# Attention scores from stacked high and low parts: two fp32r matmuls in place of one fp32 matmul on 64 rows

## The chip, the cores and the metric

The kernel runs on one core of one Trainium2 chip. The metric is the device time of one execution in microseconds (us), as the median of the runs of a kernel; less is better.

## What is computed

Two layers of a diffusion backbone over 256 context tokens and 256 latent tokens of width 1024. The even layer runs differential softmax attention (4 heads, two score maps of 64 features per head) beside a gated linear attention (GLA, 4 heads, forward and backward); the odd layer runs a gated scan (HGRN2); each layer ends in a SwiGLU feed-forward. The part that the change touches is this, for each head:

```python
aq = rms_norm(aq.reshape(Bn, L, A_HEADS, 2, A_DQK), qk_gain[0])
ak = rms_norm(ak.reshape(Bn, L, A_HEADS, 2, A_DQK), qk_gain[1])
ql = apply_axial_rope(ql, rope_cos, rope_sin)
kl = apply_axial_rope(kl, rope_cos, rope_sin)
...
s = jnp.einsum('bqhcd,bkhcd->bhcqk', q, k).astype(F32) * (A_DQK ** -0.5)
p = jax.nn.softmax(s, axis=-1)
a = (p[:, :, 0] - lam * p[:, :, 1]).astype(v.dtype)
return jnp.einsum('bhqk,bkhe->bqhe', a, v)
```

Context queries see the 256 context keys, latent queries see all 512 keys.

## The kernel before

All 512 tokens lie along the free axis and features lie on the 128 rows. Dense projections are done in three fp32r matmuls per 128x128 block of weights (`mm3`): high part of the weight times high part of the activation, high times low, low times high. A weight piece of 128x1024 arrives by one DMA, ScalarE (ACT) casts its high part (L269), VectorE (DVE) subtracts to get the low part (L270). All matmuls are recorded on one line, L117, and nearly all activations on L71, so the rows below are told apart by tile names.

The even layer's mixer is written as `qk_tile` for q and k of head 0, `gla_pair(0)`, the value projection, and then for each head `qk_tile(0, hd)`, `qk_tile(1, hd)` and `attn_head(hd)`, with pieces of the modulation (`ada`) between, then `gla_pair(1)` and four gate projections `gs` (L803). A scheduler sets the order of all instructions on each engine from this text before the run, so heads, GLA and dense work are interleaved; on the chip every engine then works through its own list in that order.

- `qk_tile` (L720 to L736) normalises a projected 128x512 tile by its root mean square (tile `qsq`, matmul with `blk64`), applies the rotation to the 256 latent tokens on VectorE (L730 to L735) and leaves the tile in fp32. Rows 0 to 63 are score map 0, rows 64 to 127 are score map 1. Each of the eight q and k tiles has its own buffer, tags `x0` to `x7`, which held the input tokens before and will hold them again (`load_x`) for the residual.
- `attn_head` (L742 to L778) goes over context and latent queries (`s`), two blocks of 128 queries (`qb`) and two score maps (`c`). A score tile is one matmul on the 64 rows of its map, into a PSUM bank of which there are two (tag `s`). VectorE takes the maximum (L757), ScalarE the exponential with its sum (tile `p`), VectorE combines both maps (L765, L766), TensorE transposes (`t_ps`, L770) and multiplies with the values (`oa_ps`).
- `head_post` (tiles `hsq`, `ms_ps`, L606) normalises a head's output: square on ScalarE, a sum over rows on TensorE (`ms_ps`), Ln and Exp on ScalarE, a product on VectorE. There is one `hsq` buffer for all eight heads.
- The gates `gs` pass through Silu only after every Exp and Ln before them (class `Act`), because the two need different function tables; a table load stands between. Then `ob` is multiplied by `gs` (L811), split into high and low parts (`oH`, `oL`, L628 and L629) and multiplied with the output weights. The output projection goes over the four attention heads first and then over the four GLA heads.

Of the kernel before, what the change touches and what calls it, by code (L numbers as in the profile page):

```python
# [10 lines left out]
F32 = mybir.dt.float32  # L11
F32R = mybir.dt.float32r
U32 = mybir.dt.uint32
AF = mybir.ActivationFunctionType
ALU = mybir.AluOpType
# [3 lines left out]
P = 128  # L19
# [3 lines left out]
T = 512  # L23
# [27 lines left out]
def hybrid_kernel(ctx: ExitStack, tc: tile.TileContext, A, out, dbg=None):  # L51
    nc = tc.nc
    PE, V = nc.tensor, nc.vector
# [34 lines left out]
    S = Act()  # L88

    def pool(es, name, bufs, **kw):  # L90
        kw.setdefault("reuse_waits", "tile")
        return es.enter_context(tc.tile_pool(name=name, bufs=bufs, **kw))

    cst = pool(ctx, "cst", 1)
    xp = pool(ctx, "xp", 1)
# [8 lines left out]
    def dma(o, i):  # L104
        nc.sync.dma_start(out=o, in_=i)
# [6 lines left out]
    def dump(name, ap):  # L112
        if dbg is not None and name in dbg:
            dma(dbg[name], ap)

    def mm(o, l, r, start, stop):
        return PE.matmul(out=o, lhsT=l, rhs=r, start=start, stop=stop)  # L117

    def mtile(name, tag):
        return pm.tile([P, 512], F32, name=name, tag=tag, bufs=1 if tag == "t" else 2)  # L120
# [5 lines left out]
    x = {}  # L126
# [127 lines left out]
    def rstd_from_ms(o, ps, n):  # L254

        S.activation(out=o, in_=ps, func=AF.Ln, scale=1.0 / n, bias=eps_t)
        S.activation(out=o, in_=o, func=AF.Exp, scale=-0.5)
# [39 lines left out]
    def dense_group(fl, outs, rhs, ks, per_bank=1, extra=0, tag="t", extra1=0):  # L297

        ada(extra, tag)
        ada1(extra1)  # L300
        for i, k in enumerate(ks):
            for j, o in enumerate(outs):
                wH, wL = fl.nxt()
                mm3(o, wH, wL, rhs[k][0], rhs[k][1], i == 0 and j % per_bank == 0,
                    i == len(ks) - 1 and j % per_bank == per_bank - 1)
# [48 lines left out]
    def dtile():  # L354
        return pd.tile([P, 512], F32, name="d", tag="d")
# [242 lines left out]
    def head_post(pp, o, src, n, gain, tag):  # L598

        sq = pp.tile([P, n], F32, name="hsq", tag="hsq", bufs=1)  # L600
        S.activation(out=sq, in_=src, func=AF.Square)
        ms = mtile("ms_ps", tag)
        mm(ms[:, 0:n], ones, sq, True, True)
        rsd = sq
        rstd_from_ms(rsd, ms[:, 0:n], P)
        V.scalar_tensor_tensor(out=o, in0=src, scalar=gain, in1=rsd, op0=ALU.mult, op1=ALU.mult)  # L606
# [110 lines left out]
    qT = {}  # L717
    kT = {}

    def qk_tile(which, hd, ps=None):  # L720
        if ps is None:
            ps = dtile()
            dense_group(fl, [ps], h, range(KT))
        rsd = ppool.tile([P, T], F32, name="qsq", tag="qsq", bufs=1)
        S.activation(out=rsd, in_=ps, func=AF.Square)
        ms = dtile()
        mm(ms, blk64, rsd, True, True)
        rstd_from_ms(rsd, ms, 64)
        t = xp.tile([P, T], F32, name=f"qk{which}{hd}", tag=f"x{2 * hd + which}")
        V.scalar_tensor_tensor(out=t, in0=ps, scalar=qkg[:, which:which + 1], in1=rsd, op0=ALU.mult, op1=ALU.mult)  # L730
        sh = ppool.tile([P, 256], F32, name="sh", tag="sh")
        V.stream_shuffle(out=sh, in_=t[:, 256:512], mask=[(i + 16) % 32 for i in range(32)])
        V.tensor_tensor(out=sh, in0=sh, in1=rope[:, 1, :], op=ALU.mult)
        V.tensor_tensor(out=t[:, 256:512], in0=t[:, 256:512], in1=rope[:, 0, :], op=ALU.mult)
        V.tensor_tensor(out=t[:, 256:512], in0=t[:, 256:512], in1=sh, op=ALU.add)  # L735
        return t  # L736

    def put_vA(t, ps):
        vA[t] = bigp.tile([P, 512], F32, name=f"vA{t}")
# [2 lines left out]
    def attn_head(hd):  # L742
        q, k = qT[hd], kT[hd]
        oa = bigp.tile([P, T], F32, name=f"oa{hd}")
        for s in range(2):
            nk = 2 + 2 * s
            nkeys = nk * P
            aT = ppool.tile([P, nk, 256], F32, name="aT", tag=f"aT{s}", bufs=1)
            for qb in range(2):
                q0 = s * 256 + qb * P  # L750
                st = ppool.tile([P, 6], F32, name="st", tag="st")
                pr = []
                for c in range(2):
                    r = slice(64 * c, 64 * c + 64)
                    sp_ = mtile("s_ps", "s")
                    mm(sp_[:, 0:nkeys], q[r, q0:q0 + P], k[r, 0:nkeys], True, True)
                    V.tensor_reduce(out=st[:, c:c + 1], in_=sp_[:, 0:nkeys], axis=AX.X, op=ALU.max)  # L757
                    V.tensor_scalar(out=st[:, c:c + 1], in0=st[:, c:c + 1], scalar1=-0.125, scalar2=None, op0=ALU.mult)
                    pt = ppool.tile([P, 512], F32, name=f"p{c}", tag=f"p{c}")
                    S.activation(out=pt[:, 0:nkeys], in_=sp_[:, 0:nkeys], func=AF.Exp, scale=0.125,  # L760
                                 bias=st[:, c:c + 1], accum_out=st[:, 2 + c:3 + c])
                    pr.append(pt)
                V.reciprocal(out=st[:, 4:6], in_=st[:, 2:4])
                V.tensor_scalar(out=st[:, 5:6], in0=st[:, 5:6], scalar1=neglam, scalar2=None, op0=ALU.mult)
                V.tensor_scalar(out=pr[0][:, 0:nkeys], in0=pr[0][:, 0:nkeys], scalar1=st[:, 4:5], scalar2=None, op0=ALU.mult)  # L765
                V.scalar_tensor_tensor(out=pr[0][:, 0:nkeys], in0=pr[1][:, 0:nkeys], scalar=st[:, 5:6],  # L766
                                       in1=pr[0][:, 0:nkeys], op0=ALU.mult, op1=ALU.add)
                tp = mtile("t_ps", "t")
                for kt in range(nk):
                    PE.transpose(tp[:, kt * P:(kt + 1) * P], pr[0][:, kt * P:(kt + 1) * P], ident)  # L770
                S.copy(out=aT[:, 0:nk, qb * P:(qb + 1) * P],
                       in_=tp[:, 0:nkeys].rearrange("p (a b) -> p a b", a=nk))
            o = mtile("oa_ps", "t")
            for kt in range(nk):
                mm(o[:, 0:256], vA[kt][:, hd * P:(hd + 1) * P], aT[:, kt, :], kt == 0, kt == nk - 1)
            S.copy(out=oa[:, s * 256:(s + 1) * 256], in_=o[:, 0:256])
        head_post(ppool, oa, oa, T, sgain, "t")
        return oa  # L778

    oa = {}  # L780
    qT[0] = qk_tile(0, 0, pss[4])
    kT[0] = qk_tile(1, 0, pss[5])
    gla_pair(0)
    dense_tokens(A["w_even_av"], h, put_vA)
    ada(2, "d")
    oa[0] = attn_head(0)
    for hd in range(1, 4):
        ada(1, "d")
        qT[hd] = qk_tile(0, hd)
        kT[hd] = qk_tile(1, hd)  # L790
        ada(1, "d")
        oa[hd] = attn_head(hd)
    dump("q1", qT[1])
    dump("oa1", oa[1])
    gla_pair(1)
    dump("ob1", ob[1])
# [138 lines left out]
    qs = bigp.tile([P, KT, 256], F32, name="qs")  # L935
# [365 lines left out]
```

## Time and profile before

| | us |
|---|---|
| median of 3 runs | 1174.69 |
| lowest and highest run | 1173.56, 1174.72 |
| the profiled execution | 1171.33 |
| its span in the trace | 1169.6 |
| TensorE (PE) busy | 1146.2 (98%) |
| PE weight loads (PEld) busy | 982.8 (84%) |
| VectorE (DVE) busy | 794.5 (68%) |
| ScalarE (ACT) busy | 546.6 (47%) |

PE's busy time is a union of modelled intervals, each with the latency of its matmul, so 98% does not mean that the array works at its peak. In the timeline the difference between the starts of two neighbouring matmuls tells what one really takes. The even layer's mixer with the attention lies between about 90 and 345 us of the span.

### The profile page before, as it was taken

To read this page: it belongs to the slowest core of one execution; us is meant where nothing else is said; L and a number is where in the kernel's file an instruction comes from. 1 tells how busy PE (TensorE), PEld (TensorE's weight loads), DVE (VectorE), ACT (ScalarE), POOL (GpSimd) and SP (SyncE) were. 2 spreads that over 40 slices of the span, in tenths; PEclk is the share of its full clock that TensorE was granted. 3 is DMA by queue.
4 is the path that set the end of the run, shared out by engine and by line. 5 is a ranking of instruction groups with operands and counts; after the bars stand their busy time and mean duration, and the time that the engine had idled before them with its cause. 6 is when DMAs were issued, how large, how long until landed. Compare 5 with 4: busy or idle time off the path is not lost. (4 is left out here: it accounts for less than half of the span.)

```text
span 1169.6 us, 21851 instructions
## 1 busy us (share of the span) xinstructions
PE 1146.2 (98%) x8954; PEld 982.8 (84%) x8954; DVE 794.5 (68%) x1671; ACT 546.6 (47%) x952; POOL 0.2 (0%) x4
## 2 busy tenths in 40 slices
PE   8999999999999999999999999999999998999998
PEld 6777665666889888888888889999898988999998
DVE  3537856985767767666677637869899976655663
ACT  5436546754435222212222325958778865433432
POOL 0000000000000000000000000000000000000000
PEclk9999989999999999999999999999999999999999
DMA  9531432234423555555776422342221234555552
GB/s 356 211 116 36 146 127 82 100 127 146 178 74 105 167 178 171 159 174 179 252 238 232 161 90 70 129 145 92 73 91 61 87 127 129 183 191 178 185 181 91
DMA packets 50021, 170.19 MB, mean 146 GB/s; under 512 B 6528, under 2 KB 8064, under 8 KB 49792
## 3 DMA queue, kind: packets, MB, share of 16 engines
q1 hardware_dynamic: 49920, 168.79, 43.2%
q8 instruction: 70, 1.15, 0.4%
q14 instruction: 31, 0.25, 0.1%
HBM read 167.72 MB, written 1.05 MB: 144 GB/s over the span
## 5 line engine op out<-in xcount | busy, mean ns | idle before, releaser
L269 ACT CAST wH<-w 128x1024 fp32r<-128x1024 f32 x212 | 222.2, 1049 | 410.2 <-PE d L117 314.0
L117 PE MATMUL d<-hL,wH 128*128 128x256 f32 (+1 forms) x1152 | 386.7, 336 | 2.5 <-DVE hL L387 2.5
L117 PE MATMUL d<-hH,wH 128*128 128x256 f32 (+1 forms) x1152 | 382.4, 339 | 5.6 <-ACT hH L71 4.1
L117 PE MATMUL d<-hH,wL 128*128 128x256 f32 (+1 forms) x1152 | 385.3, 335 | 0.0
L270 DVE TENSOR_TENSOR wL<-w,wH 128x1024 fp32r<-128x1024 f32 x212 | 258.6, 1221 | 124.7 <-ACT wH L269 122.0
L117 PEld LDWEIGHTS d<-hH,wH 128*128 128x128 f32 x1152 | 218.3, 191 | 32.0 <-ACT hH L71 4.9
L117 PEld LDWEIGHTS d<-hL,wH 128*128 128x128 f32 x1152 | 220.6, 191 | 25.0 <-DVE hL L387 3.3
L117 PEld LDWEIGHTS d<-hH,wL 128*128 128x128 f32 x1152 | 220.1, 191 | 21.5
L117 PE MATMUL d<-gL,wH 128*128 128x256 f32 (+1 forms) x374 | 121.8, 327 | 0.0
L117 PE MATMUL d<-gH,wL 128*128 128x256 f32 (+1 forms) x374 | 121.7, 327 | 0.0
L117 PE MATMUL d<-gH,wH 128*128 128x256 f32 (+1 forms) x374 | 121.7, 327 | 0.0
L227 DVE SCALAR_TENSOR_TENSOR jk<-ada_w,scb 128x1024 bf16<-128x1024 f32 x80 | 97.7, 1222 | 2.2 <-DMA ada_w<-in_w_ada 0.8
L882 DVE TENSOR_TENSOR fs<-fs,d 128x256 f32<-128x256 f32 (+1 forms) x46 | 24.6, 536 | 77.4 <-PE d L117 75.8
L117 PEld LDWEIGHTS d<-gL,wH 128*128 128x128 f32 x374 | 71.1, 190 | 6.1
L117 PEld LDWEIGHTS d<-gH,wL 128*128 128x128 f32 x374 | 71.1, 190 | 6.0
L117 PEld LDWEIGHTS d<-gH,wH 128*128 128x128 f32 x374 | 71.0, 190 | 6.0
L117 PE MATMUL d<-wH,hH 128*128 128x256 f32 (+1 forms) x192 | 61.9, 323 | 0.0
L117 PE MATMUL d<-wL,hH 128*128 128x256 f32 (+1 forms) x192 | 61.6, 322 | 0.0
L117 PE MATMUL d<-wH,hL 128*128 128x256 f32 (+1 forms) x192 | 61.5, 321 | 0.0
L825 DVE SCALAR_TENSOR_TENSOR x<-d,modt,x 128x256 f32<-128x256 f32 x64 | 28.5, 480 | 42.4 <-PE d L117 42.4
L71 ACT ACTIVATE QK<-QK 128x512 f32<-128x512 f32 x72 | 42.6, 628 | 2.4 <-DVE QK L493 2.1
L117 PEld LDWEIGHTS a<-QK 128*32 128x32 f32 (+5 forms) x1408 | 33.8, 118 | 10.1 <-issue 6.3
(216 smaller groups left out, 1461.1 us busy)
## 6 DMA issues: line engine op xcount, KB each, us to landing
w<-in_w_ffn_in SPq DMA_DIRECT2D x88, 512.0 KB, 3.4
ada_w<-in_w_ada SPq DMA_DIRECT2D x80, 512.0 KB, 4.2
w<-in_w_ffn_out SPq DMA_DIRECT2D x44, 512.0 KB, 3.4
ada_w<-in_w_ada SPq DMA_DIRECT2D x8, 1024.0 KB, 9.4
w<-in_w_even_a SPq DMA_DIRECT2D x16, 512.0 KB, 4.8
w<-in_w_odd_f SPq DMA_DIRECT2D x16, 512.0 KB, 3.3
x<-in_xT SPq DMA_DIRECT2D x16, 256.0 KB, 3.7
w<-in_w_out_even SPq DMA_DIRECT2D x8, 512.0 KB, 3.5
```

The lines of the kernel that those rows point to most:

```text
L71: ins = nc.scalar.activation(**kw)
L117: return PE.matmul(out=o, lhsT=l, rhs=r, start=start, stop=stop)
L227: ins = V.scalar_tensor_tensor(out=jk, in0=w1[0], scalar=1.0, in1=scb[:, v, :], op0=ALU.mult, op1=ALU.mult, accum_out=modt[:, l, m, dt, v: ...
L269: S.copy(out=wH, in_=w)
L270: ins = V.tensor_tensor(out=wL, in0=w, in1=wH, op=ALU.subtract)
L825: tail[0] = V.scalar_tensor_tensor(out=xt[:, lo:hi], in0=ps[:, lo:hi], scalar=mods[l, m, k][:, v:v + 1], in1=xt[:, lo:hi], op0=ALU.mult, o ...
L882: V.tensor_tensor(out=s[:, lo:hi], in0=s[:, lo:hi], in1=pu, op=ALU.mult)
```

## The change

`qk_tile` no longer returns one fp32 tile. For q it makes, for each score map `c`, a 128-row fp32r tile `qs`: the high part (ACT cast) in the map's own 64 rows and the low part (DVE subtraction) in the other 64. For k it makes two tiles for each map: `kh` with the high part in both halves and `kl` with the low part in both halves. A score tile is then `qs` times `kh` plus `qs` times `kl`, two fp32r matmuls over all 128 rows, into the same PSUM bank: all four products of high and low parts are summed.

The tags move too. The fp32 tile has tag `x6` (q) or `x7` (k) for every head, and `qs`, `kh` and `kl` have tags `x0` to `x5`, again for every head: one buffer each where there was one per head.

```diff
-        t = xp.tile([P, T], F32, name=f"qk{which}{hd}", tag=f"x{2 * hd + which}")
+        t = xp.tile([P, T], F32, name=f"qk{which}{hd}", tag=f"x{6 + which}")
...
-        return t
+        parts = []
+        for c in range(2):
+            own, far = (slice(0, 64), slice(64, 128))[::1 - 2 * c]
+            if which == 0:
+                a = xp.tile([P, T], F32R, name=f"qs{c}", tag=f"x{c}")
+                S.copy(out=a[own], in_=t[own])
+                V.tensor_tensor(out=a[far], in0=t[own], in1=a[own], op=ALU.subtract)
+                parts.append(a)
+            else:
+                a = xp.tile([P, T], F32R, name=f"kh{c}", tag=f"x{2 + 2 * c}")
+                b = xp.tile([P, T], F32R, name=f"kl{c}", tag=f"x{3 + 2 * c}")
+                for r in (own, far):
+                    S.copy(out=a[r], in_=t[own])
+                for r in (own, far):
+                    V.tensor_tensor(out=b[r], in0=t[own], in1=a[own], op=ALU.subtract)
+                parts.append((a, b))
+        return parts
...
-                    r = slice(64 * c, 64 * c + 64)
                     sp_ = mtile("s_ps", "s")
-                    mm(sp_[:, 0:nkeys], q[r, q0:q0 + P], k[r, 0:nkeys], True, True)
+                    for i in range(2):
+                        mm(sp_[:, 0:nkeys], q[c][:, q0:q0 + P], k[c][i][:, 0:nkeys], i == 0, i == 1)
```

A debug dump of `qT[1]`, which this build doesn't make, goes as well. The scheduler sets a new order for the mixer; later parts stand as they stood. Three places of it matter below.

**The scores.** On TensorE, the last scores of head 0 (numbers tell buffers apart). Before:

```order
L117 MATMUL s_ps<-qk_875,qk_862 128x512
L117 MATMUL d<-hH_625,wH 128x512
L117 MATMUL d<-hL_626,wH 128x512
L117 MATMUL d<-hH_625,wL 128x512
L117 MATMUL s_ps<-qk_875,qk_862 128x512
```

Now:

```order
L117 MATMUL s_ps<-kh_888,qs_869 128x512
L117 MATMUL s_ps<-kl_889,qs_869 128x512
L117 MATMUL s_ps<-kh_894,qs_872 128x512
L117 MATMUL s_ps<-kl_895,qs_872 128x512
L117 MATMUL o_ps<-at,vB_832 128x256
```

Each tile is two matmuls; there are 64 in all, where there were 32.

**The subtractions.** On VectorE, inside the products of `gla_pair(0)`, ahead of the first scores. Before:

```order
L500 TENSOR_TENSOR QK<-QK,qkb_688 128x256
L504 TENSOR_TENSOR QK<-QK,qkb_688 128x256
L500 TENSOR_TENSOR QK<-QK,qkb_688 128x256 x2
L504 TENSOR_TENSOR QK<-QK,qkb_688 128x256
```

Now:

```order
L500 TENSOR_TENSOR QK<-QK,qkb_688 128x256
L504 TENSOR_TENSOR QK<-QK,qkb_688 128x256
L752 TENSOR_TENSOR kl_889<-qk_881,kh_888 64x512 x2
L752 TENSOR_TENSOR kl_895<-qk_881,kh_894 64x512 x2
L500 TENSOR_TENSOR QK<-QK,qkb_688 128x256 x2
```

Four subtractions for k of head 0 stand in the queue here; the two for its q stand some 25 instructions earlier. Each further head has six of its own.

**The end of the mixer.** On TensorE, the last sum of squares `ms_ps` (that of GLA head 3) and the output projection; `oH_3202` to `oL_3215` are attention heads 0 to 3. Before, where `ms_ps` stands after 8 of the 48 matmuls on attention heads, and 40 of them follow until the first on GLA head 0:

```order
L117 MATMUL d<-oH_3206,wH 128x512
L117 MATMUL d_3255<-oH_3206,wH 128x512
L117 MATMUL ms_ps<-hsq,ones 128x512
L117 MATMUL d<-oL_3207,wH 128x512
L117 MATMUL d<-oH_3206,wL 128x512
```

Now, where `oH_3318` is attention head 3 and `oH_3323` GLA head 0; `ms_ps` twice is GLA heads 2 and 3:

```order
L117 MATMUL d_3359<-oL_3319,wH 128x512
L117 MATMUL d_3359<-oH_3318,wL 128x512
L117 MATMUL ms_ps<-hsq,ones 128x512 x2
L117 MATMUL d<-oH_3323,wH 128x512 x3
L117 MATMUL d_3359<-oH_3323,wH 128x512
L117 MATMUL d<-oL_3324,wH 128x512
```

All 48 matmuls on attention heads now stand ahead of the two sums. What ScalarE has there now (`ob_854` and `ob_855` are GLA heads 2 and 3):

```order
L71 ACTIVATE hsq<-ob_854 128x512
L269 CAST wH<-w 128x1024
L71 ACTIVATE hsq<-ms_ps,eps_t 128x512
L71 ACTIVATE hsq<-hsq 128x512
L71 ACTIVATE hsq<-ob_855 128x512
L71 ACTIVATE hsq<-ms_ps,eps_t 128x512
L71 ACTIVATE hsq<-hsq 128x512
L71 ACT_TABLE_LOAD
L71 ACTIVATE gs_3046<-gs_3046 128x512
```

The square of head 3 (`hsq<-ob_855`) stands behind Ln and Exp of head 2, as before; what moved is that TensorE's two sums stand side by side, with nothing between them.

## Rows read from the trace of the kernel before

**Rows 1.** Timeline of PE: start, duration, engine, line, tiles, count [idle before].
```profile
134.16 1.13 PE L117 MATMUL s_ps<-qk,qk 64*128 64x512 f32 x4
...
145.96 1.12 PE L117 MATMUL s_ps<-qk,qk 64*128 64x512 f32 x2
147.01 0.50 PE L117 MATMUL d<-hH,wH 128*128 128x512 f32 x1
...
157.37 0.70 PE L117 MATMUL s_ps<-qk,qk 64*128 64x256 f32 x4
...
235.28 0.70 PE L117 MATMUL s_ps<-qk,qk 64*128 64x256 f32 x2
235.91 0.41 PE L117 MATMUL d<-ada_w,sc 128*32 128x128 f32 x2
```

**Rows 2.** Timeline of PE, dense fp32r matmuls in a row, at 512 and 256 columns.
```profile
60.04 0.39 PE L117 MATMUL d<-hH,wL 128*128 128x512 f32 x1
...
62.08 0.39 PE L117 MATMUL d<-hL,wH 128*128 128x512 f32 x1
...
1019.81 0.28 PE L117 MATMUL d<-hH,wL 128*128 128x256 f32 x1
...
1023.89 0.28 PE L117 MATMUL d<-hH,wH 128*128 128x256 f32 x1
```

**Rows 3.** Lines by form, 90 to 285 us: count, busy us, mean ns, idle before.
```profile
L740 ACT COPY vA<-d 128x512 f32<-128x512 f32 x4 | 2.4, 588 | 6.4 <-PE d L117 6.3
L661 DVE TENSOR_TENSOR ls<-mn,ls 128x512 f32<-128x512 f32 x4 | 2.7, 684 | 1.6 <-ACT ls L71 1.6
L71 ACT ACTIVATE hsq<-ob 128x512 f32<-128x512 f32 x2 | 1.3, 632 | 1.4 <-DVE ob L606 1.3
```

**Rows 4.** Windows: busy us (x instructions) of PE, PEld, DVE, ACT, POOL; granted clock, DMA share, GB/s.
```profile
117.00:300.00 183.00, 177.75 (x1958) 119.29 (x1959) 134.24 (x417) 99.53 (x218) 0.00 (x0) 0.97 0.36 119
162.00:172.20 10.20, 9.22 (x32) 5.77 (x32) 7.16 (x29) 4.02 (x11) 0.00 (x0) 0.50 0.46 159
200.00:240.00 40.00, 39.55 (x360) 25.65 (x358) 37.38 (x124) 28.23 (x66) 0.00 (x0) 1.00 0.42 144
342.40:346.30 3.90, 1.12 (x7) 0.71 (x7) 3.54 (x10) 3.51 (x8) 0.00 (x0) 1.00 0.00 0
346.30:349.70 3.40, 3.40 (x18) 3.40 (x18) 3.40 (x7) 0.00 (x0) 0.00 (x0) 0.50 0.28 93
```

**Rows 5.** Timeline of PE, its two longest waits between 120 and 300 us.
```profile
140.73 0.50 PE L117 MATMUL d<-hH,wH 128*128 128x512 f32 x1 [1.17 <-DVE modt L162]
...
162.69 0.26 PE L117 MATMUL a<-qkb 64*32 64x32 f32 x2 [1.21 <-issue]
```

**Rows 6.** Timeline at the mixer's end: PE, then ACT, then DVE.
```profile
298.90 1.02 PE L117 MATMUL ms_ps<-hsq,ones 128*128 128x512 f32 x2
299.36 0.80 PE L117 MATMUL d<-oL,wH 128*128 128x512 f32 x1
...
308.87 1.07 PE L117 MATMUL d<-oH,wH 128*128 128x512 f32 x4
...
299.96 0.69 ACT L71 ACTIVATE hsq<-ms_ps,eps_t 128x512 f32<-128x512 f32 x1 [2.11 <-PE ms_ps L117]
300.68 0.63 ACT L71 ACTIVATE hsq<-hsq 128x512 f32<-128x512 f32 x1
301.33 1.28 ACT L71 ACT_TABLE_LOAD   x1
...
301.35 0.75 DVE L606 SCALAR_TENSOR_TENSOR ob<-ob,c_gains,hsq 128x512 f32<-128x512 f32 x1 [2.20 <-ACT hsq L71]
...
304.50 0.42 DVE L628 CAST oH<-ob 128x512 fp32r<-128x512 f32 x1
...
306.38 0.68 DVE L629 TENSOR_TENSOR oL<-ob,oH 128x512 fp32r<-128x512 f32 x1
```

**Rows 7.** Waits, 90 to 290 us: who waited for whom, total us, times, longest us.
```profile
DVE st L757 <- PE s_ps L117: 15.1, 11, 7.0
```

More of the change, by code (lines that the diff above doesn't have):

```diff
@@ L792, in hybrid_kernel @@
         oa[hd] = attn_head(hd)
-    dump("q1", qT[1])
     dump("oa1", oa[1])
```

## The prediction

> **What bounds the kernel now.** I read the page first: TensorE is busy nearly all the time and no other engine is. Then the windows [rows 4]: over the mixer, 117 to 300 us, PE is busy 177.75 of 183 us, VectorE 134.24, ScalarE 99.53. So TensorE sets the pace here, and a microsecond that leaves its list is worth a microsecond unless a wait takes its place. Two things in this stretch are not matmul work: PE's own waits, of which the two longest are 1.17 and 1.21 us [rows 5], and 10.2 us in which the granted clock is 0.50, the 1.2 GHz level [rows 4], after a stretch of many small matmuls. VectorE is the nearest rival: from 200 to 240 us it is busy 37.38 of 40 us [rows 4]. It also waits itself, 15.1 us in all, for score tiles [rows 7].
>
> Below I work from the profiled execution, 1171.33 us with a span of 1169.6. The median of the runs, 1174.69, lies 3.36 us above it; I carry the difference over to the median. No change can be told from a measurement of this kernel within 0.2%, about 2.3 us.
>
> **Part 1, the scores.** What a tile takes on PE is the step from its start to the next matmul's. A single 512-key tile takes 147.01 - 145.96 = 1.05 us, a single 256-key tile 235.91 - 235.28 = 0.63 us [rows 1]. Some tiles stand in pairs, one on rows 0 to 63 and one on rows 64 to 127, and these run at the same time: the row with x4 (two tiles, two records each) lasts 1.13 us at 512 keys where x2 lasts 1.12, and 0.70 at 256 where x2 lasts 0.70 [rows 1]. I counted in the timeline 3 pairs and 10 singles at 512, 4 pairs and 8 singles at 256. That is 13 x 1.05 + 12 x 0.63 = 21.2 us. New: fp32r steps are (62.08 - 60.04) / 9 = 0.227 us at 512 columns and (1023.89 - 1019.81) / 34 = 0.12 at 256 [rows 2], so 32 x 0.227 + 32 x 0.12 = 11.1 us. **Gain 10.1 us.** What a switch between 64-row and 128-row matmuls costs by itself I can't read from a row of its own; the steps above hold most of it, and I add nothing.
>
> The pairs speak against the change: it gives up a concurrency that was there. The Trainium skill, TensorEngine Tiling (Array Packing), section Key Properties, says that different tiles of the array can load weights and multiply in parallel; the trace agrees, as the x4 rows show. By that rule alone, all 32 tiles in 16 pairs, the scores would have cost 8 x 1.05 + 8 x 0.63 = 13.4 us and the gain would be 2.3; but only 14 tiles stand in pairs, so the sum goes by the rows.
>
> **Part 2, the splits.** Six subtractions and six casts per head, 24 and 24. Nearest rows: a 128x512 subtraction 0.684 us on VectorE, a 128x512 copy 0.588 on ScalarE [rows 3]; 64 rows of the same length should take as long. That is 16.4 us more for VectorE and 14.1 for ScalarE. With 134 + 16 of 183 and 100 + 14 of 183 they don't become the bound as a whole; the cover is VectorE's waiting for scores, 15.1 us [rows 7]. What isn't covered falls on PE where it already waits on VectorE and ScalarE [rows 5]: from nothing to all 16.4 us. In the new order the first head's six subtractions stand ahead of the first scores beside dense work, which needs none of them, and PE's two waits there should each grow a little. I take **1 us**, near the lower end, since both engines have slack.
>
> Sharing `x0` to `x7` among heads adds waits too: the casts of a new head wait until the last scores of the old one on that map are done. In the new order some dozens of matmuls lie between, so nothing; if that cover is gone it is a cast and two subtractions, 0.6 + 2 x 0.7 = 2 us a head, and these are in the range. The reload of `x` moves behind the last scores; the residual that reads it comes after the output projection, so nothing. No DMA is added.
>
> **Part 3, the end of the mixer.** This is where I expect the gain to go. Heads come later relative to dense work now, and all 48 matmuls on attention heads stand ahead of the last two `ms_ps`. Behind these sums hangs a chain: Ln, Exp, the table load, Silu, the product with the gate, the cast, and only then the first matmul on GLA head 0. Before, it ran from 298.90 (start of `ms_ps`) to 304.92 (end of the first cast), 6.0 us [rows 6], and PE had the 40 remaining matmuls to do from 299.36 to 308.87, 9.5 us, so it waited for none of it. Now there is nothing to do meanwhile. And the two sums stand next to each other with one `hsq` buffer: the second needs the first sum (1.02), Ln and Exp (0.69 + 0.63), the product on VectorE (0.75) and the square (0.63) [rows 3, 6], 3.7 us. From the first sum to the first GLA matmul that is 3.7 + 6.0 = 9.7 us, of which two sums, some 0.9 us each, are work: **8.0 us of waiting**. Then four matmuls on high parts (0.9 us) against 307.06 - 304.92 = 2.1 us until the low part is there [rows 6]: **1.2 us** more. Bounds: 6 us, if handing over between engines costs less than I added up, and 11.
>
> Such a wait costs clock as well. PE was busy 1.12 us of the 3.9 us from 342.4, and for the next 3.4 us, busy throughout, it had the clock at 0.50 [rows 4]: half of that lost, **1.7 us**. At worst it is as from 162 to 172.2, 9.22 us busy at the half clock, 4.6 us; at best nothing.
>
> **Sum.** -10.1 + 1 + 8.0 + 1.2 + 1.7 = +1.8 us: 1173.1 for the profiled execution, 1176.5 for the median. I forecast **no change that can be told**, leaning to slower.
>
> **The rivals.**
> 1. *Faster, by fewer weak stretches.* The 10.2 us at the half clock cost 4.6 us and the two long waits 2.4 [rows 4, 5]. In a new order the small matmuls of `gla_pair(0)` lie differently, with a few dense ones between. If both go and the splits cost nothing: 1176.5 - 1 - 4.6 - 2.4 = 1168.5; half of it, 1172.5. Against it: the same small matmuls are there, and VectorE has more to do just there.
> 2. *Slower, VectorE sets the pace inside the heads.* From 200 to 240 us it has 2.6 us left [rows 4], and one head's six subtractions are 4.1. It decides from the point where a head's `kl` is subtracted after PE has come to its scores, with no dense matmul ahead of them in the list. If half of the 16.4 us falls on PE: 1176.5 - 1 + 8.2 = 1183.7; a quarter gives 1179.6. For it: 93% busy there, and a wait of PE for VectorE at 140 us already [rows 5]. Against: PE waited hardly at all from 200 to 240 us in spite of it (39.55 busy of 40).
> 3. *The end is covered after all*, since PE comes late to the two sums and the chain starts earlier. Then PE's gain passes through: 1176.5 - 8.0 - 1.2 - 1.7 = 1165.6. Against it: within one engine's list nothing overtakes, and the chain hangs on the sums themselves.
> 4. *The change doesn't do what it says*: an fp32r matmul on stacked parts is no faster than fp32 on 64 rows. Then part 1 is 0 and the time 1186.6. The dense rows, the same kind of matmul, speak against it [rows 2].
>
> **How the numbers follow.** Forecast, 1174 to 1178.5: 0.40. Rival 1: 0.17. Rival 2: 0.34. Rival 3: 0.06. Rival 4: 0.03. Faster by over 0.2%, below 1172.3, are rival 3 and most of rival 1, 0.21; slower, above 1177.0, are rivals 2 and 4 and the forecast's upper edge, 0.43; the rest, 0.36, is within. The range for 8 in 10 leaves out rivals 3 and 4 and the far ends of 1 and 2: 1169.5 to 1183. The forecast's own range is 1174 to 1178.5.
>
> **What would show it.** Score tiles as two records stepping 0.23 or 0.12 us. The two last `ms_ps` some 3.7 us apart and the first matmul on GLA head 0 some 6 us after the second, with PE's idle time before it put down to the cast `oH`, then a wait on `oL`, and a granted clock of 0.5 for 3 us or more near 300 us. From the mixer's start to the first of the two sums PE should be about 9 us ahead of the old kernel at the same work. The forecast is wrong if PE isn't ahead there (rival 2), if the clock stays high between 150 and 175 us (rival 1), or if no gap of some 8 us is seen at the end (rival 3).

## The result, and the profile after

Medians on one chip: 1174.12 us before, **1181.07 us** after (1179.16 to 1182.82). The ratio is 1.0065, 95% interval 1.0046 to 1.0085: slower by some 7 us, clear of the noise. (Ratios here and below are those on record; the quotient of two medians can differ by some 0.001, here it is 1.0059.) The profiled executions lie further apart, 1171.33 and 1182.82 us with spans of 1169.6 and 1181.0, because the one of before was faster than the four runs behind its median and the one of after was its slowest; what follows splits these 11.4 us first, and the runs price the parts afterwards.

To split them I cut both timelines of PE at the same two matmuls: the first `g_ps` of the mixer and the first matmul on `hH` of the feed-forward. The first is 0.9 us later in the new execution, the part behind the second is 0.1 us shorter. Between them I added up the steps from one matmul's start to the next's, less the idle time marked between them. What the half clock costs is half of PE's busy time in stretches granted 0.50 (a dense step of 512 columns takes 0.43 us there, 320.23 to 320.66 us in the last rows of this section, and 0.23 at the full clock); it is taken out of the other matmuls here.

| us | scores | other matmuls, full clock | half clock | idle up to the output projection | idle after | sum |
|---|---|---|---|---|---|---|
| before | 21.7 | 220.1 | 4.6 | 5.3 | 2.0 | 253.7 |
| after | 15.5 | 217.1 | 10.0 | 11.2 | 10.6 | 264.4 |
| difference | -6.3 | -3.0 | +5.4 | +6.0 | +8.6 | +10.6 |

So the matmuls themselves became 9.3 us cheaper, and waiting and clock took 20 back. First the windows of the new kernel (columns as in [rows 4]):

```profile
117.00:300.00 183.00, 171.77 (x1973) 125.64 (x1973) 146.76 (x445) 105.59 (x230) 0.00 (x0) 0.96 0.37 122
200.00:240.00 40.00, 37.01 (x457) 27.48 (x455) 39.12 (x121) 30.24 (x68) 0.00 (x0) 1.00 0.30 101
313.20:323.44 10.24, 6.30 (x14) 4.52 (x15) 7.00 (x13) 4.97 (x7) 0.00 (x0) 0.50 0.51 212
272.24:275.65 3.41, 3.41 (x10) 2.38 (x9) 2.21 (x13) 1.52 (x5) 0.00 (x0) 0.50 0.55 208
```

Beside [rows 4], VectorE has gone from 134 to 147 us of the mixer, and from 200 to 240 us it has 0.9 us left where it had 2.6; PE, which lost 0.45 us there before, now loses 3.0. But it isn't VectorE that PE waits for in this window: 2.9 of the 3.0 us are put down to the square `qsq` on ScalarE, which is busy 30.24 of the 40 us. Two stretches at the half clock are new. PE's waits from 90 to 300 us, and in the last line those from 200 to 240 us alone (who waited for whom: total us, times, longest us):

```profile
PE d L117 <- ACT qsq L71: 4.1, 4, 1.9
PE d L117 <- DVE modt L162: 2.4, 1, 2.4
PE t_ps L788 <- issue: 1.6, 1, 1.6
PE t_ps L788 <- ACT hsq L71: 1.3, 1, 1.3
...
PE d L117 <- ACT qsq L71: 2.9, 2, 1.9
```

The two longest of these that name a releaser show the splits in the queue, ahead of what PE needs. From the timeline of the new kernel, the rows of ACT from 204.8 us and of DVE from 250.7 us, each with the row of PE that waits:

```profile
204.79 1.26 ACT L750 CAST kh<-qk 64x512 fp32r<-64x512 f32 x2
206.07 0.61 ACT L743 CAST qs<-qk 64x512 fp32r<-64x512 f32 x1
206.71 0.60 ACT L71 ACTIVATE qsq<-d 128x512 f32<-128x512 f32 x1
207.36 1.13 PE L117 MATMUL d<-qsq,c_blk 128*128 128x512 f32 x2 [1.85 <-ACT qsq L71]
...
250.71 1.39 DVE L752 TENSOR_TENSOR kl<-qk,kh 64x512 fp32r<-64x512 f32 x2
252.02 0.68 DVE L744 TENSOR_TENSOR qs<-qk,qs 64x512 fp32r<-64x512 f32 x1
252.63 0.17 DVE L162 TENSOR_REDUCE modt<-d 128x4 f32<-128x16 f32 x1
252.85 0.62 PE L117 MATMUL d<-ada_w,sc 128*32 128x128 f32 x13 [2.38 <-DVE modt L162]
```

At 250.7 us three subtractions, 2.07 us in all, stand ahead of the small `modt`, and PE waits 2.38 us for it. At 204.8 three casts stand ahead of the square `qsq`, and PE waits 1.85. `modt` belongs to the modulation, and this `qsq` to the q tile of head 3, while the casts ahead of it are those of head 2: neither needs a split. These two waits, 4.2 us of the 11.2, are the ones that I traced to splits. The other wait for a `qsq` from 200 to 240 us, 1.02 us, has GLA's activations ahead of it; the rest I did not trace. VectorE's own waiting for scores, 15.1 us in [rows 7], has shrunk meanwhile:

```profile
DVE st L775 <- PE s_ps L117: 9.2, 7, 4.1
```

And the end of the mixer, which answers to [rows 6]: rows of PE, ACT and DVE from 307 us.

```profile
306.99 1.02 PE L117 MATMUL ms_ps<-hsq,ones 128*128 128x512 f32 x2
...
308.06 0.69 ACT L71 ACTIVATE hsq<-ms_ps,eps_t 128x512 f32<-128x512 f32 x1
308.77 0.63 ACT L71 ACTIVATE hsq<-hsq 128x512 f32<-128x512 f32 x1
309.44 0.75 DVE L606 SCALAR_TENSOR_TENSOR ob<-ob,c_gains,hsq 128x512 f32<-128x512 f32 x1 [0.17 <-ACT hsq L71]
310.22 0.63 ACT L71 ACTIVATE hsq<-ob 128x512 f32<-128x512 f32 x1 [0.82 <-DVE ob L606]
310.90 1.13 PE L117 MATMUL ms_ps<-hsq,ones 128*128 128x512 f32 x2 [2.88 <-ACT hsq L71]
312.07 0.69 ACT L71 ACTIVATE hsq<-ms_ps,eps_t 128x512 f32<-128x512 f32 x1 [1.22 <-PE ms_ps L117]
312.79 0.63 ACT L71 ACTIVATE hsq<-hsq 128x512 f32<-128x512 f32 x1
313.43 1.28 ACT L71 ACT_TABLE_LOAD   x1
314.73 2.19 ACT L71 ACTIVATE gs<-gs 128x512 f32<-128x512 f32 x4
...
316.60 0.42 DVE L628 CAST oH<-ob 128x512 fp32r<-128x512 f32 x1
317.07 2.07 PE L117 MATMUL d<-oH,wH 128*128 128x512 f32 x4 [5.04 <-DVE oH L628]
319.21 0.79 PE L117 MATMUL d<-oL,wH 128*128 128x512 f32 x1
...
320.23 0.63 PE L117 MATMUL d<-oL,wH 128*128 128x512 f32 x1
320.66 0.63 PE L117 MATMUL d<-oH,wL 128*128 128x512 f32 x1
```

Two sums with nothing between, 3.9 us apart: the second waits for Ln and Exp of the first, the product on VectorE and then the next square. 6.2 us later the first matmul on a GLA head. PE idles 2.88 + 5.04 = 7.9 us where before it idled not at all, and from 313.20 to 323.44 us the clock is at 0.50: 6.30 us busy, half of it lost.

### The profile page after: what moved, and what is told of

Its sections match the earlier page's. It is cut to its first block, busy times and chain, and to the rows that moved or that the text cites. A ratio compares the mean times of both kernels' runs of the same rounds, so it can differ in the third digit from the quotient of the medians.

```text
span 1181.0 us, 21916 instructions
## 1 busy us (share of the span) xinstructions
PE 1143.0 (97%) x8954; PEld 989.1 (84%) x8954; DVE 809.4 (69%) x1695; ACT 559.2 (47%) x976; POOL 0.2 (0%) x4
```

## Experiments

Each run is set against the kernel before on the same chip. The runs come from several chips, so kernels are compared with each other by these ratios. Where a kernel "apart" is named, the end of the mixer is covered, as in the second one.

**One more buffer for a square, and two.** The same edit for one or for both of the last GLA heads:

```diff
-    def head_post(pp, o, src, n, gain, tag):
+    def head_post(pp, o, src, n, gain, tag, xtag=None):
-        sq = pp.tile([P, n], F32, name="hsq", tag="hsq", bufs=1)
+        sq = xp.tile([P, n], F32, name="hsq", tag=xtag) if xtag else pp.tile([P, n], F32, name="hsq", tag="hsq", bufs=1)
...
-            head_post(ppool, ob[2 * p + hi], ob[2 * p + hi], T, gains[:, 1:2], "a")
+            head_post(ppool, ob[2 * p + hi], ob[2 * p + hi], T, gains[:, 1:2], "a", f"x{6 + hi}" if p else None)
```

(For one: `"x7" if p and hi else None`.)

> The change, with the square of the last GLA head in a buffer of its own (tag x7, free by then), so that it no longer waits for the product of the head before. TensorE's list is the same as in the changed kernel. Theory (the end of the mixer costs 7.9 us of idle PE and 3.2 us of half clock): the 2.9 us before the last sum go, the 5.0 us behind it stay, so about 1178 us. Rival (the chain hangs on something ahead of the squares, so the idle time only moves behind the last sum): the two waits together stay at 7.9 us and the time at 1181.

Measured: ratio 1.0056 (1.0038 to 1.0075). PE at the end, in its timeline:

```profile
304.54 1.88 PE L117 MATMUL ms_ps<-hsq,ones 128*128 128x512 f32 x4
311.85 2.07 PE L117 MATMUL d<-oH,wH 128*128 128x512 f32 x4 [5.42 <-DVE oH L628]
```

The wait between the sums is gone, and the one behind them is 5.4 us: 2.5 us less in the trace, as the theory has it and not as the rival does. The timed runs moved by 0.0009, 1 us, which their intervals can't tell from 0 or from 3.

> The change, with the squares of both last GLA heads in buffers of their own (tags x6 and x7). TensorE's list is the same up to the last score; at the end the two last sums now stand behind 8 and 18 of the 48 matmuls on attention heads, so 30 matmuls of about 0.23 us, 6.8 us, cover a chain of 6.0. Theory (the end costs 11.1 us, idle and half clock together): nearly all of it goes, 1170 to 1172 us, faster than the kernel before. Rival (the scheduler moves the wait: PE comes to the sums before the squares are ready): half of it stays, 1175 to 1177. Second rival (the loss lies in the heads, where PE waits 11 us for ScalarE and VectorE): 1181.

Measured: ratio **0.9978** (0.9967 to 0.9990). The end of the mixer now, on PE:

```profile
291.76 1.02 PE L117 MATMUL ms_ps<-hsq,ones 128*128 128x512 f32 x2
...
294.93 1.02 PE L117 MATMUL ms_ps<-hsq,ones 128*128 128x512 f32 x2
...
300.40 1.19 PE L117 MATMUL d<-oH,wH 128*128 128x512 f32 x4 [0.33 <-DVE oH L628]
302.54 0.50 PE L117 MATMUL d<-oL,wH 128*128 128x512 f32 x1 [0.95 <-DVE oL L629]
```

Of 7.9 us of waiting 1.3 are left. Nothing in PE's list up to the last score moved, and idle time up to the output projection is 11.0 us, in the change 11.2. From 1.0065 to 0.9978 is 0.0087, **10.2 us** (give or take 2.6): what the end of the mixer cost. The traces show 6.6 us less waiting there and 3.2 us of half clock gone behind it, 9.8 together; they also show some 3.5 us less half clock inside the heads, in the same list of PE, which I can't lay to the edit.

> The kernel before with the same two buffers for squares. There the end of the mixer was covered already, with 40 matmuls behind the last sum, so the theory of the end expects no difference: within 0.2% of the kernel before. If the serial squares cost PE time there too, it would be faster by 1 to 3 us.

Measured: 0.9996 (0.9984 to 1.0007). The buffers are worth nothing that can be told where the end was covered already. So the kernel "apart" can be compared with the kernel before.

**Subtractions taken away.** In place of each subtraction's result the high part is used; the 24 casts and all 64 matmuls stay:

```diff
-                S.copy(out=a[own], in_=t[own])
-                V.tensor_tensor(out=a[far], in0=t[own], in1=a[own], op=ALU.subtract)
+                for r in (own, far):
+                    S.copy(out=a[r], in_=t[own])
...
-                for r in (own, far):
-                    V.tensor_tensor(out=b[r], in0=t[own], in1=a[own], op=ALU.subtract)
-                parts.append((a, b))
+                parts.append((a, a))
```

(The tile `kl` goes; q gets eight casts more, so there are 32.)

> squares_apart without the 24 subtractions: the high parts stand in place of the low parts, so the scores' low parts are left out; 64 score matmuls and 24 casts stay. Theory (the subtractions on VectorE cause PE's additional waits inside the heads): idle time of PE before the output projection falls from 11.0 us to about 5, as in the kernel before, and the time to about 6 us below squares_apart, ratio to before 0.993. Rival (the casts on ScalarE, to which the longest of these waits are put down, or the order): it stays above 9 us and the time within 2 us of squares_apart.

Measured: **0.9912** (0.9899 to 0.9925). That is 0.0066 below squares_apart, **7.7 us** (give or take 2). By the same account of PE's timeline, idle time up to the output projection falls from 11.0 to 7.6 us, at the end from 3.3 to 2.0, and the other matmuls take 1.9 us less. The time went as the theory says, the idle time only half as far. The longest wait left is again for ScalarE, which here has eight casts more:

```profile
PE d L117 <- ACT qsq L71: 2.9, 1, 2.9
```

The expectation counted the casts as unchanged, which was a slip; if eight casts cost time, the subtractions' price is above 7.7 us. The scheduler orders the heads anew in this kernel, so the 7.7 us hold what it makes of the room, too.

**The splits without their use**, with the fp32 scores of the kernel before. The edit is made to squares_apart and keeps its tags, so the fp32 tiles of q and k, which the scores read here, have one buffer each where the kernel before has one per head:

```diff
-        return parts
+        return t
...
-                    for i in range(2):
-                        mm(sp_[:, 0:nkeys], q[c][:, q0:q0 + P], k[c][i][:, 0:nkeys], i == 0, i == 1)
+                    r = slice(64 * c, 64 * c + 64)
+                    mm(sp_[:, 0:nkeys], q[r, q0:q0 + P], k[r, 0:nkeys], True, True)
```

> The kernel before (fp32 scores on 64 rows) that makes all 24 casts and 24 subtractions of the change as well, and uses none of them, with the change's tags and squares_apart's buffers. Theory (the splits cost PE time by the load they put on VectorE and ScalarE): idle time of PE before the output projection rises from 5.2 to about 11 us and the time by 6 us, ratio 1.005. Rival (they cost only where scores wait for them, and here none does): within 2 us of the kernel before. The 10 us that the new scores gain are missing here in either case.

Measured: 1.0078 (1.0063 to 1.0093), **9.1 us** slower than the kernel before, though no score waits for a split. Idle time up to the output projection rises from 5.3 to 13.5 us. PE's waits with the largest totals are for engines that are late with something else:

```profile
PE d L161 <- ACT ada_ev L159: 3.0, 3, 1.6
PE oa_ps L117 <- ACT aT L789: 2.2, 3, 1.5
PE d L117 <- ACT qsq L71: 1.9, 3, 0.8
```

Ahead of the longest of these, 1.56 us at 244.2, ScalarE has two casts `qs` of 1.25 us; ahead of the next, 1.51 us at 206.3, it has GLA's activations and the cast of a weight, and no split close by. From 200 to 240 us VectorE is busy 33.27 us, less than before [rows 4], and yet PE, busy 35.35, loses 4.7 us there: how full VectorE's window is doesn't decide it.

So the subtractions cost 7.7 us where they are taken away, and all splits 9.1 where they are added. How much of this is their place in the queues, and how much the new order that the scheduler makes around them, the runs don't separate. Nor were the shared buffers tried without the splits; in this trace no wait on the writing of `qk` (L730) is put down to scores, but they may act through the order.

**Fewer casts.** One cast of 128 rows for each q and k tile, `S.copy(out=a, in_=t)`, used for both maps and both matmuls:

> squares_apart with one cast of 128 rows for each q and k tile and no subtraction: every score tile is two fp32r matmuls of the same two casts, the low parts and the separation of the two maps are left out. Against apart_no_subtractions 16 of 24 casts go, 9.9 us of ScalarE. If the casts cost PE time as the subtractions do, some 4 us faster than apart_no_subtractions (ratio 0.988); if ScalarE has room for them, the same within 1.5 us (0.991).

There are 8 casts here against 32 in apart_no_subtractions. Measured: 0.9906 (0.9888 to 0.9923), which can't be told from it. In the profiled execution idle time up to the output projection falls further, from 7.6 to 3.8 us. What the casts cost by themselves stays open: by the interval, between nothing and some 3 us.

**Moving or saving subtractions.** Four kernels; the short edits are the line of the second subtraction for `kl`, given to another engine, or left out.

```diff
-                    V.tensor_tensor(out=b[r], in0=t[own], in1=a[own], op=ALU.subtract)
+                    (V if r == own else nc.gpsimd).tensor_tensor(out=b[r], in0=t[own], in1=a[own], op=ALU.subtract)
```

> squares_apart, with the second subtraction for each low part of k on GpSimd, which does nothing else: 8 of 24 leave VectorE. If VectorE's load makes PE's waits, they fall by 2 to 3 us, unless a subtraction takes so long on GpSimd (no row shows it) that scores wait for it: above some 3 us apiece the time rises. If GpSimd slows VectorE's work beside it, VectorE's subtractions there take longer than 0.684 us.

Measured: 1.0004 (0.9988 to 1.0020): no gain, and by the ratios 3 us slower than squares_apart (give or take 2.3; by the medians 1 us). All instructions on `kl` (count, shortest/median/longest in ns, first and last start in us, forms):

```profile
L752 POOL TENSOR_TENSOR kl<-qk,kh x8: 1424/1622/5557, 109.6 to 247.3; 64x512 fp32r<-64x512 f32 x8
L752 DVE TENSOR_TENSOR kl<-qk,kh x8: 671/687/1682, 113.3 to 251.0; 64x512 fp32r<-64x512 f32 x8
```

A subtraction took 1.4 to 1.8 us on GpSimd, and one 5.6. Six of VectorE's own took 0.67 to 0.69 us as before, the other two 1.08 and 1.68, both beside GpSimd's. Whether this made the kernel slower is not shown.

> squares_apart, with the second half of each low part of k copied by ScalarE from the first in place of a second subtraction: 8 subtractions of 0.684 us leave VectorE, 8 copies of about 0.62 come to ScalarE. If VectorE's load makes PE's waits in the heads, they fall by 2 to 3 us and the time is that much below squares_apart. If it is ScalarE's, they grow by as much. If it is the order alone, no rule.

Here the second half is `S.copy(out=b[far], in_=b[own])`. Measured: 0.9976 (0.9958 to 0.9994), no difference to squares_apart that can be told. Idle time up to the output projection fell from 11.0 to 8.6 us, and that at the end rose from 3.3 to 5.1: inconclusive.

> As squares_apart, and the second matmul of a score tile is the high part of q times the low part of k on the 64 rows of its map, without the product of the two low parts. Two subtractions per head go, 8 in all, 5.5 us of VectorE. The end of the mixer is covered too. Theory that PE's waits inside the heads come from the load on VectorE and ScalarE: they fall by about a third of 6 us, and the time is 2 us below squares_apart. Rival (they come from the order alone): the time is within 1 us of it, or moves with the order either way. Price of the mixed shapes on PE, unknown: up to 0.1 us for each of 32 tiles, 3 us the other way.

The edit keeps one tile `kl` with each map's low part in its own rows, and the second matmul is `q[c][own]` times `kl[own]`. Measured: 0.9976 (0.9963 to 0.9990), no difference either, and here a reason shows. Idle time up to the output projection fell from 11.0 to 4.4 us, and the score steps rose from 15.5 to 23.6. In PE's timeline of this kernel:

```profile
129.14 0.49 PE L117 MATMUL s_ps<-kl,qs 64*128 64x512 f32 x1
129.56 0.50 PE L117 MATMUL s_ps<-kh,qs 128*128 128x512 f32 x1
129.99 0.50 PE L117 MATMUL s_ps<-kl,qs 64*128 64x512 f32 x1
130.42 0.43 PE L117 MATMUL d<-ada_w,sc 128*32 128x128 f32 x8
```

Each step is 0.42 or 0.43 us, and in the changed kernel, in two places:

```profile
148.05 0.39 PE L117 MATMUL s_ps<-kh,qs 128*128 128x512 f32 x1
148.28 0.39 PE L117 MATMUL s_ps<-kl,qs 128*128 128x512 f32 x1
148.51 0.39 PE L117 MATMUL s_ps<-kh,qs 128*128 128x512 f32 x1
...
238.30 0.38 PE L117 MATMUL a<-qkb 64*32 64x32 f32 x19
238.61 0.50 PE L117 MATMUL s_ps<-kh,qs 128*128 128x512 f32 x1
238.95 0.40 PE L117 MATMUL s_ps<-kl,qs 128*128 128x512 f32 x1
239.28 0.31 PE L117 MATMUL a<-qkb 64*32 64x32 f32 x10
```

Among dense matmuls a step is 0.23 us; beside a matmul on a part of the array (64*32 here) it is 0.33 or 0.34. The dearer scores, 8.1 us, are enough to eat what the idle time gave back, 6.6. The last kernel therefore keeps all rows:

```diff
-                b = xp.tile([P, T], F32R, name=f"kl{c}", tag=f"x{3 + 2 * c}")
+                if c not in kls:
+                    kls[c] = xp.tile([P, T], F32R, name=f"kl{c}", tag=f"x{3 + 2 * c}")
+                    S.mul(out=kls[c][far], in_=t[own], mul=0.0)
+                b = kls[c]
...
-                for r in (own, far):
-                    V.tensor_tensor(out=b[r], in0=t[own], in1=a[own], op=ALU.subtract)
+                V.tensor_tensor(out=b[own], in0=t[own], in1=a[own], op=ALU.subtract)
```

> squares_apart, with the low parts of k only in the map's own 64 rows and zeros, written once before head 0, in the other 64: the product of the two low parts is left out, 8 of 24 subtractions go, all matmuls stay on 128 rows. Theory (subtractions cost 7.7 us in all, and the dearer scores of fewer_subtractions came from the mixed shapes): a third of 7.7, 2.6 us below squares_apart, ratio to before 0.9955, and score steps as in squares_apart, some 15.5 us in all against 23.6. Rival (what counts is the four subtractions in a row ahead of a head's scores, so the last one decides): within 1 us of squares_apart.

Measured: **0.9961** (0.9947 to 0.9975), 1165.63 against 1169.92 us: the lowest ratio of the kernels that compute the scores from both parts (like the one before it, it leaves out the product of the two low parts), faster than both the kernel before and the change. Score steps are 16.6 us against 23.6, so the dearer scores came from the mixed shapes; idle time up to the output projection is 6.7. It lies 0.0017, 2 us, below squares_apart; the intervals overlap, so theory and rival aren't told apart.

## Why the prediction was right in its range and wrong in a term

The forecast was 1176.5 us, no change that can be told; measured were 1181.07, inside the range but above the forecast's own, 1174 to 1178.5, and a change that can be told. One of the prediction's own signs points to the step that failed: at the first of the two last sums PE should have been about 9 us ahead at the same work. From the mixer's first `g_ps` (91.03 us before, 91.96 after) the old kernel takes 217.8 us to the first matmul on a GLA head, at 308.87 [rows 6]; the new one takes 215.0 to the first of the two sums, at 306.99, and the two sums of 0.9 us are all that it still has to do by then. That is 1.0 us ahead. Step by step:

- **Part 1, forecast -10.1 us: near in sum, wrong inside.** Matmuls are 9.3 us cheaper by the account of the trace. But the new score steps add up to 15.5 us, not 11.1, so the scores gave 6.3. "What a switch between 64-row and 128-row matmuls costs by itself ... I add nothing" was the wrong choice, and the price came from dense rows [rows 2]. Of the 4.4 us too few, 1.8 lie in the matmuls of 512 columns, where 14 of 32 stand beside a tile of another shape and step 0.33 or 0.34; 2.6 lie in those of 256, where 14 of 32 steps are about 0.12 and the others 0.19 to 0.52. The other matmuls made up for most of it: at full clock they take 3.0 us less, which nothing in the prediction foresaw, so that the sum came out near is in part luck. Some of these 3.0 us are the same switch from its other side: before, the six dense matmuls just ahead of a 64-row score tile stepped 0.32 or 0.33 us, now seven of the nine ahead of a score step 0.22 to 0.24.
- **Part 2, forecast +1 us: this is the term that failed.** It measured 6.0 us of added idle time in the trace, and 7.7 and 9.1 us in the two runs that come nearest to isolating it. "The cover is VectorE's waiting for scores, 15.1 us" was the wrong step. That waiting did shrink, from 15.1 to 9.2 us, but covering needs room at the right place: a split in the queue delays whatever stands behind it, on ScalarE as on VectorE, and `qsq` and `modt` had PE waiting. No busy share told this beforehand; VectorE's 37.38 of 40 us [rows 4] lie in the window where PE's new waits are for ScalarE.
- **Rival 2** came nearest: half of 16.4 us, its price of 8.2, is close to what the runs gave, though the half was a choice and not worked out, so the match is in part luck. Its point of decision was off: it isn't a head's own scores that wait for `kl`, but other work. No wait of a score for `kl` is in the new trace, and before_with_splits has the loss where no score uses the splits.
- **Buffer sharing and the reload, forecast 0.** No wait in the new profile is put down to them; they were not tried by themselves.
- **Part 3, forecast 8.0 + 1.2 + 1.7 = 10.9 us: right.** The sums stand 3.9 us apart (3.7), the chain behind them takes 6.2 (6.0), and PE idles 7.9 us. The wait on `oL` came to less than 0.1 us, since the four matmuls ahead of it ran at the half clock; that clock cost 3.2 us, not 1.7. squares_apart prices the whole at 10.2 us.
- **Clock elsewhere.** The stretch of 10.2 us near 160 us is there as before, and the one at 272 us is new and cost 1.7 us. But with the same list of PE up to the last score, squares_apart and one_more_square had 3.41 us near 160 and 3.41 near 250 us in place of both, so the order alone doesn't set these stretches. I can't lay the new one to the change, and whether rival 1's 4.6 us go or stay can differ from execution to execution.

Set end to end, the runs split the whole: -10.3 us from the kernel before to apart_no_subtractions, +7.7 to squares_apart, +10.2 to the change, +7.6 in all, the ratio of 1.0065. This is a split and no check, since each run starts where the last one ends, and the -10.3 hold other order and other waits beside the scores. With Rival 2's 8.2 us for Part 2 the forecast would have been 1183.7, 9.0 above its median of before where 7.0 were measured.

## What to carry to other kernels

Work given to another engine is not covered by that engine's idle time elsewhere: look at the place in the queue where it lands, and ask what stands behind it and who waits for that. When the critical engine becomes faster, look at the end of the stage: a chain that had cover may lose it, and here two spare buffers for the squares were worth about as much as the faster matmuls. Take the price of a matmul from a row with the neighbours it will have.

## What the runs showed of the hardware

- **A change of tile shape costs both matmuls beside it.** For fp32r at 512 columns and the full clock, between matmuls on the same tile shape 15 of 18 steps in the changed kernel were 0.23 to 0.24 us; the other three, each next to a transpose or an fp32 matmul of that shape, took about 0.31. (With a smaller shape on one side all 14 took 0.33 or 0.34, but those neighbours are fp32 as well.) In fewer_subtractions, a score on 128 rows after a dense matmul and ahead of one on 64 rows took 0.32 or 0.33 (all 3), and with another shape on both sides all 22 took 0.42 or 0.43, the 8 with nothing but fp32r around them like the rest. The Trainium skill, TensorEngine Tiling (Array Packing), section Key Properties, says that changing the tiling mode drains TensorE; steps longer by about 0.1 us on each side agree with it, though no run shows the drain itself.
- **Halving the rows saves no time on VectorE and ScalarE.** A 64x512 subtraction took 0.684 us, as the 128x512 one in [rows 3]; a 64x512 cast took 0.617, the 128x512 copy 0.588.
- **GpSimd and VectorE can hinder each other.** With eight subtractions on GpSimd, VectorE's own took 1.08 and 1.68 us in two cases, 1.01 and 1.61 of them beside one on GpSimd, and 0.67 to 0.69 in the other six, three of which also ran beside one. The Trainium skill, SBUF — State Buffer, section on the two separate sides, says that a VectorE instruction with two inputs in SBUF and a GpSimd instruction that reads SBUF shut each other out, and that the one that starts first goes on. The two long ones started while one of GpSimd's ran, and two of the three just before one, which agrees; the third started inside the GpSimd subtraction of 5.6 us and kept its time, which does not (the profile's spans on GpSimd are rough).
